# Two projections of a Trainium2 kernel: the subtraction that splits their weight chunks moves from VectorE to GpSimd

## The chip, the core and the metric

The kernel runs on one core of a Trainium2 chip. The metric is device time in microseconds (us) of one execution. The engines of the core work side by side, each through its own queue in order: TensorE (PE, matrix products, with weight loads shown as PEld), VectorE (DVE), ScalarE (ACT), GpSimd (POOL) and SyncE (SP, whose queue issues the loads from the chip's memory). They wait for each other through semaphores. SBUF is the working memory, PSUM holds what TensorE adds up.

## The reference

The program is a whole small network on 256 tokens of width 1024: two layers of attention with a feed-forward part, then a second block of two layers (mixer, cross attention, an expert layer with 128 x 128 experts). The change lies in the first of these mixers, the "even mixer". Its input `hn` is projected once and cut up; two of the parts go through a causal convolution over four tokens and a SiLU:

```python
def even_mixer(hn, w_in, w_out, ...):
    proj = hn @ w_in
    z, xbc, dt_raw, xm, og, ig, fg = jnp.split(proj, [o1, o2, o3, o4, o5, o6], axis=-1)
    y_a = ssd_mixer(z, xbc, dt_raw, ...)      # xbc: 1536 columns
    y_b = mlstm_mixer(xm, og, ig, fg, ...)    # xm: 1024 columns
    return jnp.concatenate([y_a, y_b], axis=-1) @ w_out

def ssd_mixer(...):
    xbc = jax.nn.silu(causal_conv(xbc, conv_w, conv_b))
    ...
def mlstm_mixer(...):
    xc = jax.nn.silu(causal_conv(xm, conv_w, conv_b))
    ...
```

The two projections with convolutions are `xbc` and `xm`. All of it is float32.

## The kernel before

Every large product is done in three passes. Each float32 operand is split into a rounded part `hi` and a rest `lo` (`split`, L295): ScalarE copies the operand to `hi` in TensorE's rounding format (L297), and then `lo` = operand minus `hi` is computed (L298) by the engine that is passed as `eng`, VectorE where none is passed. `mm3` (L311) issues three matmuls for each piece: `hi` by `hi` (L313), `hi` by the other side's rest (L314), and `lo` by `hi` (L315). So the third matmul is the first that needs `lo`.

Weights come in chunks of 128 x 1024 floats (512 KB). `chunk` (L300) loads one into `raw` (three buffers, L303), and splits it into `hi` and `lo` (three buffers each). A `raw` buffer is free for the next load once the subtraction has read it; `hi` and `lo` are free once TensorE has used them.

`lin_b_steps` (L344) goes through the blocks of 128 output columns: a PSUM bank, a chunk, 24 matmuls (8 pieces of the input by 3), and then a `consume` function on the result. It takes `eng` and passes it to `chunk`. For the expert layer, `eng=nc.gpsimd` is passed already (L1715, L1752).

In `even_mixer` (L1191) the first projection, `xbc`, has 12 blocks. Each is consumed by `conv` (L1177): ScalarE copies the bank to `xpad` (L1182), whose first three columns GpSimd clears (L1181), VectorE does one tensor_scalar (L1185) and three scalar_tensor_tensor steps (L1187), ScalarE a tanh (L1188), and VectorE the last product (L1189) into `xb`. Its core:

```python
nc.vector.tensor_scalar(acc, xpad[:, 3:S + 3], w(3), w("b"), op0=OP.mult, op1=OP.add)
for j in range(3):
    nc.vector.scalar_tensor_tensor(out=acc, in0=xpad[:, j:j + S], scalar=w(j), in1=acc, op0=OP.mult, op1=OP.add)
```

Between the blocks stand the softplus of small columns (L1163 to L1174) and, in `ssd` (L1260), the decay matrices `MT` (L1311) and `cme` (L1303). When all 12 are through, TensorE transposes `xb` (L1322). The projection `z` follows, then the output of the scan, and a group norm over it (L1371 to L1382) whose row goes through a small matmul (L1380, bank `rb`).

In `mlstm` (L1386) the second projection, `xm`, has 8 blocks. Each is split straight from PSUM (`xmh`, `xml`), goes through the same `conv`, and the result is split as well (`xch`, `xcl`). After it come four chunks of `og`, and the products for q, k and v (`qkp`, `vp`), whose first weight chunk is again split by VectorE. All these share four PSUM banks.

The order of the instructions in each queue is set by a scheduler when the kernel is built: it starts from the order in the code and moves an instruction forward where it expects an engine to be free. So an instruction can stand ahead of one that was written earlier. SyncE's queue holds the loads in the order of the chunks.

Of the kernel before, what the change touches and what calls it, by code (L numbers as in the profile page):

```python
# [197 lines left out]
class Net:  # L198
# [992 lines left out]
    def even_mixer(self, xp, hT):  # L1191
        nc, a = self.nc, self.a
        c = self.tables(xp, "U", "selGT")
        ident = self.ident

        sw = xp.tile([P, 192], F32, name="sw")
        nc.sync.dma_start(out=sw, in_=a["ev_sm"].rearrange("p k n -> p (k n)"))
        swh = xp.tile([P, 192], F32R, name="swh")
        swl = xp.tile([P, 192], F32R, name="swl")
        self.split(sw, swh, swl)  # L1200
        ps = self.bank("sps")
        for k in range(8):
            self.mm3(ps[0:24, 0:S], swh[:, k * 24:k * 24 + 24], swl[:, k * 24:k * 24 + 24], hT[0][:, k], hT[1][:, k], k == 0, k == 7)
        yT = self.pair(xp, "yT", 16)
        st = ExitStack()
        sp_ = st.enter_context(self.tc.tile_pool(name="ssd", bufs=1))
        xb = sp_.tile([P, 12, S], F32, name="xb")
        xbc = self.lin_b_steps(hT, a["ev_xbc"], lambda b, ps: self.conv(sp_, ps, "sconv", b, xb[:, b]),
                               [8, 9, 10, 11, 0, 1, 2, 3, 4, 5, 6, 7], bank="psb")
        self.take(xbc, 2)  # L1210
        smT = xp.tile([24, S], F32, name="smT")
        nc.scalar.copy(out=smT, in_=ps[0:24, 0:S])
        tps = self.bank("smp")
        for t in range(2):
            nc.tensor.transpose(tps[:, t * 24:t * 24 + 24], smT[:, t * P:t * P + P], ident[0:24, 0:24])
        sm = xp.tile([P, 2, 24], F32, name="smv")
        nc.vector.tensor_tensor(out=sm, in0=tps[:, 0:48].rearrange("p (t n) -> p t n", t=2),
                                in1=self.row["smb"][:, None, :].to_broadcast([P, 2, 24]), op=OP.add)
        x20 = xp.tile([P, 2, 20], F32, name="x20")
        nc.vector.tensor_copy(x20[:, :, 0:16], sm[:, :, 0:16])  # L1220
        nc.vector.tensor_scalar(x20[:, :, 16:20], sm[:, :, 16:20], -1.0, None, op0=OP.mult)
        spl = self.softplus(xp, x20.rearrange("p t n -> p (t n)"), 40).rearrange("p (t n) -> p t n", t=2)
        dt = spl[:, :, 0:16]
        na = xp.tile([P, 16], F32, name="na")
        nc.scalar.activation(out=na, in_=self.row["alog"], func=AF.Exp)
        nc.vector.tensor_scalar(na, na, -1.0, None, op0=OP.mult)
        lg = xp.tile([P, 2, 20], F32, name="lg")
        nc.vector.tensor_tensor(out=lg[:, :, 0:16], in0=dt, in1=na[:, None, :].to_broadcast([P, 2, 16]), op=OP.mult)
        nc.vector.tensor_scalar(lg[:, :, 16:20], spl[:, :, 16:20], -1.0, None, op0=OP.mult)
        self.take(xbc, 3)  # L1230
        cps = self.bank("cps")
        for t in range(2):
            nc.tensor.matmul(cps[:, t * 20:t * 20 + 20], lhsT=c["U"], rhs=lg[:, t], start=True, stop=True)
        nc.tensor.matmul(cps[:, 40:60], lhsT=self.ones, rhs=lg[:, 0], start=True, stop=True)
        cs = xp.tile([P, 3, 20], F32, name="cs")
        nc.vector.tensor_copy(cs, cps[:, 0:60].rearrange("p (t n) -> p t n", t=3))

        acc = [[self.bank("eacc") for _ in range(2)] for _ in range(2)]

        def project():  # L1240
            for kt in range(16):
                hi, lo = self.chunk(a["ev_out"][kt].rearrange("p k n -> p (k n)"), 1024)
                for t in range(2):
                    for n in range(2):
                        self.mm3(acc[t][n], yT[0][:, kt, t * P:t * P + P], yT[1][:, kt, t * P:t * P + P],
                                 hi[:, n * 512:n * 512 + 512], lo[:, n * 512:n * 512 + 512], kt == 0, kt == 15)
                yield 1
        out = project()
        self.gain_ahead("norm_xattn_2_0")
        with st:  # L1250
            self.ssd(sp_, c, hT, dt, cs, lg, yT, xb, xbc)
        with ExitStack() as st:
            sp_ = st.enter_context(self.tc.tile_pool(name="mls", bufs=1))
            self.mlstm(sp_, c, hT, sm, cs, yT, out)
        self.take(out)
        for t in range(2):
            for n in range(2):
                self.add_h(n, t, acc[t][n])
# [127 lines left out]
    def mlstm(self, pl, c, hT, sm, cs, yT, out):  # L1386
        nc, a = self.nc, self.a
# [10 lines left out]
        with self.tc.tile_pool(name="mlx", bufs=1) as px:  # L1398
            xc = self.pair(px, "xc", 8)
            xm = self.pair(px, "xm", 8)  # L1400

            def cxm(b, ps):
                self.split(ps, xm[0][:, b], xm[1][:, b])
                y = px.tile([P, S], F32, tag="xcf", name="xcf", bufs=2)
                self.conv(px, ps, "mconv", b, y)
                self.split(y, xc[0][:, b], xc[1][:, b])
            self.lin_b(hT, a["ev_xm"], cxm, bank="psb")
            self.take(og, 4)
            for hp in range(2):
                for s, dst, scl in (("q", qT, 1.0), ("k", kT, 1.0 / 16)):  # L1410
                    hi, lo = self.chunk(a[f"ml_w{s}"][hp].rearrange("p h k n -> p (h k n)"), 1024)
                    for j in range(2):
                        h = 2 * hp + j
                        ps = self.bank("qkp")
                        for e in range(2):
                            for k in range(2):
                                o = (j * 2 + k) * 256 + e * P
                                self.mm3(ps[:, e * S:e * S + S], hi[:, o:o + P], lo[:, o:o + P], xc[0][:, 2 * h + k], xc[1][:, 2 * h + k],
                                         k == 0, k == 1)
                        nc.scalar.mul(out=dst[:, 2 * h:2 * h + 2].rearrange("p e n -> p (e n)"), in_=ps, mul=scl)  # L1420
                hi, lo = self.chunk(a["ml_wv"][hp].rearrange("p h k n -> p (h k n)"), 1024)
                for j in range(2):
                    h = 2 * hp + j
                    ps = self.bank("vp")
                    for t in range(2):
                        for k in range(2):
                            o = (j * 2 + k) * 256
                            sl = slice(t * P, t * P + P)
                            self.mm3(ps[:, t * S:t * S + S], xm[0][:, 2 * h + k, sl], xm[1][:, 2 * h + k, sl], hi[:, o:o + 256],
                                     lo[:, o:o + 256], k == 0, k == 1)  # L1430
                    nc.vector.tensor_copy(v[:, :, h, 0:256], ps.rearrange("p (t n) -> p t n", t=2))
# [522 lines left out]
```

## Time and profile before

| | us |
|---|---|
| three timed runs | 3366.87, 3373.19, 3374.19 (median 3373.19) |
| the profiled execution, its own time | 3366.57 |
| its span, first to last instruction | 3364.8 |
| TensorE busy in it | 3272.0 (97%) |
| VectorE busy | 2243.8 (67%) |
| ScalarE busy | 1755.5 (52%) |
| GpSimd busy | 322.3 (10%) |

The profile is one execution. A "busy" engine has an instruction under way; an instruction that has begun and can't go on counts as busy too. "Idle before" is the time in which an engine waited ahead of an instruction, with the one that released it. The granted clock is TensorE's, as a share of its full 2.4 GHz. Shares over the whole span are averages over many stages, so a change in one stage has to be read in that stage, by window.

### The profile page before, as it was taken

To read this page: it belongs to the slowest core of one execution; us is meant where nothing else is said; L and a number is where in the kernel's file an instruction comes from. 1 tells how busy PE (TensorE), PEld (TensorE's weight loads), DVE (VectorE), ACT (ScalarE), POOL (GpSimd) and SP (SyncE) were. 2 spreads that over 40 slices of the span, in tenths; PEclk is the share of its full clock that TensorE was granted. 3 is DMA by queue.
4 is the path that set the end of the run, shared out by engine and by line. 5 is a ranking of instruction groups with operands and counts; after the bars stand their busy time and mean duration, and the time that the engine had idled before them with its cause. 6 is when DMAs were issued, how large, how long until landed. Compare 5 with 4: busy or idle time off the path is not lost. (4 is left out here: it accounts for less than half of the span.)

```text
span 3364.8 us, 54101 instructions
## 1 busy us (share of the span) xinstructions
PE 3272.0 (97%) x20874; PEld 2883.3 (86%) x20874; DVE 2243.8 (67%) x3999; ACT 1755.5 (52%) x3219; POOL 322.3 (10%) x197
## 2 busy tenths in 40 slices
PE   8999999999999999999999999999999999999999
PEld 7678998677998888898988999988889898899998
DVE  7676556666557776599955555567649996555555
ACT  4555445554446554345944444456444595444444
POOL 0000000000000000374000000000027600000000
PEclk9999999999999999999999999999999999999999
DMA  6435666444555345453255555555545415555555
GB/s 194 143 126 185 221 200 201 141 143 167 188 186 182 124 155 187 154 170 122 82 192 187 189 187 187 187 198 170 182 144 169 139 63 188 189 187 188 188 188 175
DMA packets 161108, 569.49 MB, mean 169 GB/s; under 512 B 18257, under 2 KB 23761, under 8 KB 159826
## 3 DMA queue, kind: packets, MB, share of 16 engines
q1 hardware_dynamic: 160562, 565.91, 50.4%
q8 instruction: 163, 2.67, 0.3%
q14 instruction: 95, 0.78, 0.1%
q10 hardware_dynamic: 288, 0.13, 0.0%
HBM read 556.53 MB, written 9.44 MB: 168 GB/s over the span
## 5 line engine op out<-in xcount | busy, mean ns | idle before, releaser
L298 DVE TENSOR_TENSOR lo<-raw,hi 128x1024 fp32r<-128x1024 f32 (+2 forms) x868 | 1056.0, 1218 | 723.9 <-ACT hi L297 718.8
L297 ACT CAST hi<-raw 128x1024 fp32r<-128x1024 f32 (+1 forms) x978 | 1020.7, 1044 | 916.2 <-issue 213.2
L313 PE MATMUL pacc<-hi,pwh 128*128 128x512 f32 x1024 | 404.3, 395 | 0.1
L315 PE MATMUL pacc<-hi,pwl 128*128 128x512 f32 x1024 | 403.6, 394 | 0.0
L314 PE MATMUL pacc<-lo,pwh 128*128 128x512 f32 x1024 | 402.8, 393 | 0.0
L313 PE MATMUL aps<-xTh,hi 128*128 128x256 f32 x1248 | 351.6, 282 | 1.9 <-ACT G L1796 1.9
L314 PE MATMUL aps<-xTl,hi 128*128 128x256 f32 x1248 | 351.5, 282 | 0.0
L315 PE MATMUL aps<-xTh,lo 128*128 128x256 f32 x1248 | 350.2, 281 | 0.0
L313 PE MATMUL ps<-xTh,hi 128*128 128x256 f32 x1008 | 289.3, 287 | 3.7 <-DVE xTl L298 2.8
L298 POOL TENSOR_TENSOR lo<-raw,hi 128x1024 fp32r<-128x1024 f32 x110 | 271.4, 2470 | 213.6 <-ACT hi L297 210.0
L314 PE MATMUL ps<-xTl,hi 128*128 128x256 f32 x1008 | 287.9, 286 | 1.2 <-DVE xTl L298 1.2
L315 PE MATMUL ps<-xTh,lo 128*128 128x256 f32 x1008 | 287.7, 286 | 0.0
L297 ACT CAST pwh<-G 128x256 fp32r<-128x256 f32 x256 | 103.8, 406 | 343.1 <-DVE G L1801 205.8
L313 PEld LDWEIGHTS aps<-xTh,hi 128*128 128x128 f32 x1248 | 234.7, 188 | 8.5 <-ACT G L1796 2.3
L314 PEld LDWEIGHTS aps<-xTl,hi 128*128 128x128 f32 x1248 | 234.7, 188 | 6.9
L315 PEld LDWEIGHTS aps<-xTh,lo 128*128 128x128 f32 x1248 | 234.7, 188 | 0.0
L315 PEld LDWEIGHTS pacc<-hi,pwl 128*128 128x128 f32 x1024 | 192.5, 188 | 45.5 <-DVE pwl L298 0.3
L313 PEld LDWEIGHTS pacc<-hi,pwh 128*128 128x128 f32 x1024 | 192.7, 188 | 38.7 <-ACT pwh L297 1.0
L314 PEld LDWEIGHTS pacc<-lo,pwh 128*128 128x128 f32 x1024 | 193.2, 189 | 38.0
L448 POOL TENSOR_TENSOR r<-v,mhalf 128x1 f32<-128x1 f32 x24 | 19.7, 824 | 1987.6 <-DVE v L446 1987.6
L313 PE MATMUL fps<-fTh,hi 128*128 128x256 f32 x704 | 198.5, 282 | 0.6 <-ACT fTh L297 0.4
L314 PE MATMUL fps<-fTl,hi 128*128 128x256 f32 x704 | 198.3, 282 | 0.3
(673 smaller groups left out, 7161.4 us busy)
## 6 DMA issues: line engine op xcount, KB each, us to landing
raw<-in_pu_dram SPq DMA_DIRECT2D x256, 512.0 KB, 3.3
raw<-in_pv_dram SPq DMA_DIRECT2D x256, 512.0 KB, 3.3
raw<-in_wbg_dram SPq DMA_DIRECT2D x48, 512.0 KB, 3.6
raw<-in_ffg_dram SPq DMA_DIRECT2D x44, 512.0 KB, 3.4
raw<-in_ffu_dram SPq DMA_DIRECT2D x44, 512.0 KB, 3.4
raw<-in_ffd_dram SPq DMA_DIRECT2D x44, 512.0 KB, 3.8
raw<-in_win_dram SPq DMA_DIRECT2D x36, 512.0 KB, 3.6
raw<-in_pwq_dram SPq DMA_DIRECT2D x32, 512.0 KB, 3.3
```

Source lines behind the costliest of these rows:

```text
L297: self.nc.scalar.copy(out=hi, in_=src)
L298: (eng or self.nc.vector).tensor_tensor(out=lo, in0=src, in1=hi.bitcast(F32), op=OP.subtract)
L313: mm(ps, lhsT=lh, rhs=rh, start=start, stop=False)
L314: mm(ps, lhsT=lh, rhs=rl, start=False, stop=False)
L315: mm(ps, lhsT=ll, rhs=rh, start=False, stop=stop)
L448: nc.gpsimd.tensor_tensor(out=r, in0=v, in1=self.mhalf[:, :1], op=OP.pow)
```

## The change

Both calls pass `eng=nc.gpsimd`. Nothing else is edited.

```diff
         xbc = self.lin_b_steps(hT, a["ev_xbc"], lambda b, ps: self.conv(sp_, ps, "sconv", b, xb[:, b]),
-                               [8, 9, 10, 11, 0, 1, 2, 3, 4, 5, 6, 7], bank="psb")
+                               [8, 9, 10, 11, 0, 1, 2, 3, 4, 5, 6, 7], bank="psb", eng=nc.gpsimd)
...
-            self.lin_b(hT, a["ev_xm"], cxm, bank="psb")
+            self.lin_b(hT, a["ev_xm"], cxm, bank="psb", eng=nc.gpsimd)
```

So 20 subtractions (12 and 8) change their engine, and the scheduler sets the order anew around them. On GpSimd, at the start of the first projection (`xpad` is the convolution's input, cleared in its first columns; `r` and `w` belong to the norm ahead):

```order
 L489 TENSOR_TENSOR w<-u,mhalf 128x1 x2
-L1181 MEMSET xpad 128x3 x12
+L1181 MEMSET xpad 128x3 x2
+L298 TENSOR_TENSOR lo<-raw,hi 128x1024 x4
+L1181 MEMSET xpad 128x3
+L298 TENSOR_TENSOR lo<-raw,hi 128x1024
+L1181 MEMSET xpad 128x3
+L298 TENSOR_TENSOR lo<-raw,hi 128x1024 x2
```

The queue that held only the 12 clearings now has the subtractions between them, four of them ahead of the third clearing.

On VectorE at the same place (`cacc` is the convolution's sum, `smv`, `x_10623` and `sp_a` are the softplus's columns, `mTl` an earlier split):

```order
 L298 TENSOR_TENSOR mTl<-raw,mTh 128x1024 x2
-L298 TENSOR_TENSOR lo<-raw,hi 128x1024 x2
+L1185 TENSOR_SCALAR cacc<-xpad,cl 128x256
 L1217 TENSOR_TENSOR smv<-smp,rw 128x48
+L1187 SCALAR_TENSOR_TENSOR cacc<-xpad,cl,cacc 128x256
 L1220 COPY x_10623<-smv 128x2x16
 L1221 TENSOR_SCALAR x_10623<-smv 128x2x4
-L298 TENSOR_TENSOR lo<-raw,hi 128x1024
-L1185 TENSOR_SCALAR cacc<-xpad,cl 128x256
```

The first convolution moves ahead, into the places of the subtractions.

On VectorE in the group norm ahead of the second projection (`gn_*` are its rows, `rb` the bank with its result):

```order
 L1371 TENSOR_SCALAR gn_v<-vps 2x256
-L298 TENSOR_TENSOR lo<-raw,hi 128x1024
 L1374 TENSOR_TENSOR gn_u<-gn_y 2x256
 L1375 TENSOR_TENSOR gn_u<-gn_u,gn_v 2x256
 L1376 TENSOR_SCALAR gn_u<-gn_u 2x256
-L298 TENSOR_TENSOR lo<-raw,hi 128x1024
 L1377 TENSOR_TENSOR gn_y<-gn_y,gn_u 2x256
```

The first two subtractions of the second projection leave this chain; they now stand in GpSimd's queue.

## Rows read from the trace of the kernel before

**Rows 1.** the page: busy us (share) xcount; costliest groups as busy, mean ns | idle
```profile
PE 3272.0 (97%) x20874; PEld 2883.3 (86%) x20874; DVE 2243.8 (67%) x3999; ACT 1755.5 (52%) x3219; POOL 322.3 (10%) x197
L298 POOL TENSOR_TENSOR lo<-raw,hi 128x1024 fp32r<-128x1024 f32 x110 | 271.4, 2470 | 213.6 <-ACT hi L297 210.0
```

**Rows 2.** busy us by window; columns window, length, PE, PEld, DVE, ACT, POOL, clock, DMA
```profile
1069.00:1125.40 56.40, 52.77 (x436) 51.50 (x437) 51.99 (x114) 33.48 (x78) 1.45 (x10) 1.00 0.48 159
1170.80:1210.30 39.50, 34.01 (x230) 30.85 (x231) 37.58 (x83) 23.59 (x50) 0.96 (x10) 0.96 0.42 147
```

**Rows 3.** timeline, GpSimd: start, us, engine line op, [idle before <-releaser]
```profile
1414.32 2.38 POOL L298 TENSOR_TENSOR lo<-raw,hi 128x1024 fp32r<-128x1024 f32 x1 [0.49 <-ACT hi L297]
...
2594.13 2.40 POOL L298 TENSOR_TENSOR lo<-raw,hi 128x1024 fp32r<-128x1024 f32 x1 [0.36 <-ACT hi L297]
2596.98 2.56 POOL L298 TENSOR_TENSOR lo<-raw,hi 128x1024 fp32r<-128x1024 f32 x1 [0.45 <-ACT hi L297]
```

**Rows 4.** timeline, VectorE, beside those three
```profile
1415.04 0.29 DVE L1871 MAX8 G<-rsc 128x8 f32<-128x128 f32 x1
...
2594.18 2.43 DVE L1909 TENSOR_SCALAR G<-G 128x128 uint32<-128x128 uint32 x1
2597.21 2.49 DVE L1921 SCALAR_TENSOR_TENSOR G<-G 128x128 f32<-128x128 f32 x1
```

**Rows 5.** line L1921: count, duration ns min/median/max, first and last start
```profile
L1921 DVE SCALAR_TENSOR_TENSOR G<-G x128: 275/282/2497, 1490.7 to 2671.9; 128x128 f32<-128x128 f32 x128
```

**Rows 6.** VectorE groups, 1069 to 1125.4 us: xcount | busy, mean ns | idle
```profile
L298 DVE TENSOR_TENSOR lo<-raw,hi 128x1024 fp32r<-128x1024 f32 x15 | 18.3, 1221 | 3.8 <-ACT hi L297 3.7
L1281 DVE COPY cb<-cbp 128x512 f32<-128x512 f32 x1 | 0.7, 683 | 0.0
L1273 DVE COPY bt<-btp 128x256 f32<-128x256 f32 x1 | 0.4, 417 | 0.0
```

**Rows 7.** VectorE groups, 1170.8 to 1210.3 us
```profile
L298 DVE TENSOR_TENSOR lo<-raw,hi 128x1024 fp32r<-128x1024 f32 x11 | 13.4, 1219 | 0.0
L1382 DVE SCALAR_TENSOR_TENSOR xb<-xb,cl,rb 128x256 f32<-128x256 f32 x8 | 3.4, 476 | 1.3 <-PE rb L1380 1.3
L298 DVE TENSOR_TENSOR xml<-psb,xmh 128x256 fp32r<-128x256 f32 x8 | 3.2, 417 | 0.0
```

**Rows 8.** timeline, VectorE, last convolution of the first projection
```profile
1124.96 0.43 DVE L1189 SCALAR_TENSOR_TENSOR xb<-xpad,cacc 128x256 f32<-128x256 f32 x1
```

**Rows 9.** timeline, TensorE, the transposes that read all convolutions
```profile
1128.07 2.04 PE L1322 MATMUL xsp<-cst,xb 128*128 128x128 f32 x16
```

**Rows 10.** timeline, VectorE, group norm ahead of the second projection
```profile
1167.78 0.28 DVE L1376 TENSOR_SCALAR gn_u<-gn_u 2x256 f32<-2x256 f32 x1
1167.98 1.21 DVE L298 TENSOR_TENSOR lo<-raw,hi 128x1024 fp32r<-128x1024 f32 x1
1169.12 0.41 DVE L1377 TENSOR_TENSOR gn_y<-gn_y,gn_u 2x256 f32<-2x256 f32 x1
```

**Rows 11.** timeline, ScalarE, same place
```profile
1166.75 1.04 ACT L297 CAST hi<-raw 128x1024 fp32r<-128x1024 f32 x1
```

**Rows 12.** timeline, TensorE, same place
```profile
1169.67 0.67 PE L1380 MATMUL rb<-gn_y,cst 2*128 2x256 f32 x2 [0.92 <-DVE gn_y L1377]
```

**Rows 13.** timeline, VectorE, end of the second projection
```profile
1210.21 1.22 DVE L298 TENSOR_TENSOR lo<-raw,hi 128x1024 fp32r<-128x1024 f32 x1
```

**Rows 14.** timeline, TensorE, the matmul that reads that tile
```profile
1213.30 0.28 PE L315 MATMUL qkp<-xch,lo 128*128 128x256 f32 x1
```

**Rows 15.** TensorE waits, 1060 to 1130 us: us in total, times, longest
```profile
PE psb L315 <- DVE lo L298: 3.6, 3, 1.8
```

**Rows 16.** TensorE waits, 1165 to 1215 us
```profile
PE psl L314 <- DVE lo L298: 2.3, 1, 2.3
PE psl L313 <- ACT xpad L1182: 1.7, 1, 1.7
```

**Rows 17.** busy us by window, 1200 to 1220 us
```profile
1200.00:1220.00 20.00, 19.25 (x105) 16.45 (x105) 13.76 (x23) 11.78 (x20) 0.20 (x2) 0.91 0.58 192
```

## The prediction

> **What bounds the kernel now.** I read the page first, for the share of each engine. TensorE is busy 97% of the span, GpSimd 10%; one subtraction of a weight chunk on GpSimd, as it stands elsewhere in this kernel, takes 2.47 us [rows 1]. So the kernel is near TensorE's limit, and a change elsewhere counts only where TensorE waits. Then I cut out the two stretches that are touched, by window. In stretch A, from the first matmuls of the first projection to the end of its last convolution (1069.0 to 1125.4 us), TensorE is busy 52.77 of 56.40 us and VectorE 51.99; in stretch B, from the second projection until the last convolution there is split (1170.8 to 1210.3 us), 34.01 and 37.58 of 39.50 us [rows 2]. In both, VectorE is as full as TensorE or fuller. That is the reader's first finding: relief for VectorE would matter here, and a further load on it would as well. TensorE's waits name its share: 3.6 us for `lo` in A [rows 15]; in B 2.3 us for `lo` and 1.7 us for a bank that a ScalarE copy has to clear [rows 16], after which the granted clock of 1200 to 1220 us is 0.91, so some matmuls ran at the lower of the two levels [rows 17].
>
> Last I looked up how GpSimd's subtraction and VectorE get on where they already run together, in the expert layer. A VectorE tensor_scalar of 128x128 begins 0.05 us after a GpSimd `lo` and takes 2.43 us, to that subtraction's end; the next one of that kind under a `lo`, a scalar_tensor_tensor, takes 2.49 us [rows 3, 4]. Over its 128 executions that scalar_tensor_tensor has a median of 0.282 us and a maximum of 2.497 us [rows 5]. It isn't slower by a share: it stands still until GpSimd is done. A MAX8, which reads one tensor, ran in 0.29 us in the middle of another `lo` [rows 3, 4].
>
> **The change part by part.** Twelve chunks of the first projection and eight of the second lose a VectorE subtraction of 1.22 us each [rows 6, 7] and get one of 2.47 us on GpSimd [rows 1]. No DMA, no ScalarE cast and no matmul is added. The wait of each L315 matmul, and the release of each `raw` buffer, moves from VectorE to GpSimd.
>
> The question is what VectorE can do during those 2.47 us. The convolution (L1185 to L1189), the softplus, the products with `cb` and `ex`, and the splits of `yT` and `xc` read two tensors from SBUF or are tensor_scalars from SBUF to SBUF: the kinds that stood still in rows 4. Some operations read PSUM and at most one tensor in SBUF (`cb`, `bt`, `xml`, L1382). No row shows one of these under a GpSimd `lo`; MAX8 is the nearest, so I let them run, and keep the other case as a bound.
>
> Stretch A. VectorE's 51.99 us less 12 x 1.221 = 14.65 us leaves 37.3 us [rows 2, 6]. Of this 1.5 us read PSUM (`cb` 0.7, `bt` 0.4 [rows 6], and two small ones of 0.2). So 35.8 us want the shared path, and GpSimd wants 12 x 2.47 = 29.6 us of it. One after the other that is 65.4 us from 1068.9: 1134.3 us. In between the path is idle at times: VectorE was idle 4.4 us of this stretch before, mostly at its start, where the first two GpSimd subtractions now fit in; I add 2 of the 4.4. The last convolution then ends near 1136.3 instead of 1125.4 us [rows 8], 10.9 us later. TensorE needs it at 1128.07, at the transposes of L1322 [rows 9], so 2.7 us are swallowed: +8.2 us. Ends: if nothing stands still, two of the three waits on `lo` go (2.7 of 3.6 us) and the first chunk's `lo` comes 1.2 us later: -1.5 us. If all 12 hold VectorE for their whole length, 12 x 1.25 = 15 us, and the 2.7 us are gone for other reasons: +15 us.
>
> Ahead of stretch B the group norm loses two subtractions from VectorE's row. The second one stood between L1376 and L1377, from 1167.98 for 1.21 us [rows 10]. Without it L1377 could start 1.1 us sooner. But ScalarE's cast for that chunk ends at 1167.79 [rows 11], GpSimd starts then or behind L1376 at 1168.0, and L1377, which reads two SBUF tensors, stands still to 1170.4 and ends at 1170.8 instead of 1169.53. The matmul of L1380 waits for it already [rows 12]: +1.3 us. If it slips in first: -0.9 us, the wait in rows 12.
>
> Stretch B. VectorE's 37.58 us less six subtractions, 6 x 1.22 = 7.3 us, leaves 30.3 us, of which 3.4 (L1382) and 3.2 us (`xml`) read PSUM [rows 2, 7]. So 23.7 us want the path, and GpSimd 6 x 2.47 = 14.8 us: 38.5 us if those 6.6 us all fit beside GpSimd, 45.1 us if none does, against 37.58: +0.9 to +7.5, middle 4.2 us. At the end VectorE's `lo` of the next projection is done at 1211.4 [rows 13], and TensorE reads it at 1213.30 [rows 14], so 1.9 us are swallowed. Together 1.3 + 4.2 - 1.9 = +3.6 us. Ends: -7 us without any standstill (next part but one), and 1.3 + 7.5 = +8.8 us.
>
> What the VectorE rows say of the order: the scheduler moves convolutions forward into the places that are left. In GpSimd's queue the clearing of `xpad` now stands behind subtractions, so the first convolution of B waits until the fifth subtraction is done. This is inside the sum above, since the path is held in that time anyway.
>
> One rule of the notes bears on this. The Trainium skill, "SBUF — State Buffer", section "Who interferes with whom", says that VectorE shares its second SBUF port with GpSimd, that an operation with two SBUF inputs or in a two-port mode and a GpSimd operation that reads SBUF exclude each other for the whole instruction, and that one with a single SBUF input doesn't contend. The trace agrees with the first two (2.43 and 2.49 us in rows 4) and with the third for MAX8. By its last part alone stretch B would be at its lower value, 0.9 instead of 4.2 us, and the sum at +8.5 us.
>
> **Sum.** 8.2 + 3.6 = 11.8, some +12 us. The profiled execution took 3366.57 us by its own time, with a span of 3364.8 us; the three timed runs lie at 3366.87, 3373.19 and 3374.19 us, their median 6.6 us above the profiled one. On the profiled execution the sum gives 3378.4, on the median 3385.0; I take the middle, 3382 us. Between TensorE's stretches and the end everything hangs on the buffers and not on a fixed hour, so I let the delay go through to the end whole.
>
> **The rivals.**
> Faster: the standstill of rows 4 belongs to the operations of that layer, and the convolution's don't stand still. Then TensorE's waits go: 1.5 us in A; in B 0.9 (rows 12), 2.3 and 1.7 (rows 16), and the clock's 9% of 20 us, 1.8 us (rows 17), less a `lo` that is late for want of a cast, 1 us: about 7 us there. 8 us in all, 3362 us. For it: B's waits are VectorE's lateness, and 20 x 1.22 us are much relief. Against it: rows 4 and 5. The place is the convolution in both stretches; the point from which it decides is a subtraction that holds VectorE for less than half of its 2.47 us, since VectorE paid 1.22 us for it before.
>
> Hidden: VectorE is late, but three weight buffers and four PSUM banks let TensorE run ahead, and the transposes at L1322 can be reached with less delay than I think; the relief in B pays for A. 0 to +5 us, 3372 us. For it: TensorE reached L1322 2.7 us after the last convolution as it was [rows 8, 9], and it is idle only 3.6 of 56.4 us in A [rows 2]. Against it: the transposes need every convolution, and 10.9 us are four times that slack.
>
> Worse: GpSimd has its next operands ready whenever it ends, so VectorE gets an operation or two between subtractions, casts that stand behind ScalarE's tanh come late, and TensorE's longer waits end at the lower clock as in rows 17. Then A costs 15 and B 8.8 us, and two more such falls of the clock 3.6 us: +27 us, 3397 us.
>
> **How the numbers follow.** About 0.2%, 6.7 us, is what a measurement of this kernel can tell from no change. Forecast (the shared path decides, +5 to +22 us): 0.55. Worse: 0.13. Hidden: 0.19. Faster: 0.13. So faster 0.13, same 0.19, slower 0.68. The range that holds 8 in 10: from 3365, which leaves most of the faster case out, to 3400 us, which takes the worse one in; the forecast's own range is 3375 to 3392 us.
>
> **What would show it.** Right: under a GpSimd `lo` the convolution's operations in the new profile have durations up to some 2.5 us beside a usual 0.4 to 0.5; the last L1189 of A ends near 1136; TensorE has a new wait of 5 to 9 us at L1322 and a wait for `gn_y` near 2 us. Wrong: L1187 keeps its mean near 0.48 us in A; then the faster rival holds. If the means rise but TensorE shows no wait at L1322, the delay is hidden. If TensorE waits for GpSimd's `lo` at most chunks, the queue order on GpSimd and ScalarE is the bound, not the path.

## The result and the profile after

The changed kernel takes 3395.95 us in the median of five runs (3391.03 to 3401.22), the kernel before 3373.19 us in five runs beside it. The ratio is 1.0078, with an interval of 1.0066 to 1.0090: 26 us slower. The profiled execution has a span of 3389.3 us against 3364.8, 24.5 us more. The two stretches and the sign are the ones that the prediction named, and the time lies inside its whole range (3365 to 3400 us). But the loss is more than twice the +12 us of the sum and above the forecast's own +5 to +22 us, and the first stretch costs more than twice what it said.

I split the spans by five marks on TensorE: the first matmul of the first projection, the first and the last of the eight decay blocks (`csb`, L1305), the transposes of L1322 and the first `rwb` matmul.

| us between marks | before | after | more |
|---|---|---|---|
| first matmul to first `csb` | 23.90 | 38.31 | 14.4 |
| first to last `csb` | 28.48 | 35.61 | 7.1 |
| last `csb` to L1322 | 6.80 | 6.80 | 0 |
| L1322 to `rb` (L1380), with the group norm | 41.60 | 42.72 | 1.1 |
| `rb` to `rwb`, with stretch B | 60.41 | 64.17 | 3.8 |

The first three rows are stretch A: 59.18 before, 80.72 after. It begins 0.9 us earlier and the rest of the span is 1.1 us shorter, so 26.4 of the marks become the 24.5 of the span.

Stretch A of the kernel after, by window (window, length, busy us of TensorE, weight loads, VectorE, ScalarE, GpSimd, then clock, DMA share and GB/s); it ends with the last convolution:

```profile
1068.02:1146.31 78.29, 60.42 (x438) 57.59 (x439) 60.26 (x102) 32.86 (x78) 29.98 (x22) 0.87 0.35 115
```

Against [rows 2], VectorE has 12 subtractions less and is busy 8 us longer, and TensorE's mean clock fell from 1.00 to 0.87. VectorE's groups in this stretch (count, busy us, mean ns, idle before and who ended it) show where VectorE's time went, first those of before, 1069 to 1125.4 us, then those of after, 1068 to 1146.3 us:

```profile
L1187 DVE SCALAR_TENSOR_TENSOR cacc<-xpad,cl,cacc 128x256 f32<-128x256 f32 x36 | 17.2, 479 | 0.3
...
L1185 DVE TENSOR_SCALAR cacc<-xpad,cl 128x256 f32<-128x256 f32 x12 | 4.9, 409 | 0.0
```

```profile
L1187 DVE SCALAR_TENSOR_TENSOR cacc<-xpad,cl,cacc 128x256 f32<-128x256 f32 x36 | 23.4, 650 | 1.1
L1185 DVE TENSOR_SCALAR cacc<-xpad,cl 128x256 f32<-128x256 f32 x12 | 16.4, 1370 | 11.7 <-ACT xpad L1182 11.7
...
L1169 DVE TENSOR_TENSOR sp_z<-sp_z 128x40 f32<-128x40 f32 x1 | 2.4, 2415 | 0.0
```

The same 48 steps of the convolution take 39.8 us where they took 22.1, and one 128x40 step of the softplus takes 2.4 us. One decay block of after, the engines together (start, us, engine, line, operation, idle before):

```profile
1118.47 0.42 ACT L1188 ACTIVATE xpad<-cacc 128x256 f32<-128x256 f32 x1 [3.49 <-DVE cacc L1187]
1118.79 1.03 ACT L297 CAST hi<-raw 128x1024 fp32r<-128x1024 f32 x1
...
1119.90 2.38 POOL L298 TENSOR_TENSOR lo<-raw,hi 128x1024 fp32r<-128x1024 f32 x1 [0.34 <-ACT hi L297]
...
1120.13 2.31 DVE L1185 TENSOR_SCALAR cacc<-xpad,cl 128x256 f32<-128x256 f32 x1 [0.78 <-ACT xpad L1182]
...
1122.54 1.01 DVE L1187 SCALAR_TENSOR_TENSOR cacc<-xpad,cl,cacc 128x256 f32<-128x256 f32 x2
1123.47 0.68 DVE L1311 TENSOR_TENSOR MT<-MT,cb 128x512 f32<-128x512 f32 x1
1124.07 0.48 DVE L1187 SCALAR_TENSOR_TENSOR cacc<-xpad,cl,cacc 128x256 f32<-128x256 f32 x1
1124.64 0.42 ACT L1188 ACTIVATE xpad<-cacc 128x256 f32<-128x256 f32 x1 [3.50 <-DVE cacc L1187]
```

Read it as a ring of 6.17 us (1118.47 to 1124.64): tanh, the cast that stands behind it in ScalarE's queue, GpSimd's subtraction, VectorE's scale held until the subtraction's end at 1122.28, then the convolution and the next tanh. In each ring neither GpSimd nor VectorE has anything to do for 0.54 us under the tanh and for 0.56 us until the cast is done; between the two VectorE makes the block's last product (L1189).

TensorE's waits in after, 1055 to 1150 us (us in total, times, longest), against the 3.6 us of [rows 15]:

```profile
PE cbp L1279 <- DVE xb L1189: 6.1, 1, 6.1
PE psb L315 <- POOL lo L298: 3.4, 3, 2.0
PE psb L313 <- DVE cs L1236: 3.2, 1, 3.2
PE csb L1305 <- ACT xpad L1182: 2.2, 1, 2.2
PE cso L1299 <- ACT xpad L1182: 2.0, 1, 2.0
```

The two longest lie ahead of the first decay block. `cbp` needs four finished convolutions; the other waits for a PSUM bank that the copy `cs` clears. That copy ran 1.06 us after its matmuls before (1089.27 against 1088.21) and 11 us after them now (1100.26 against 1089.30), behind nine steps of the convolutions, three of which were held for 2.3 to 2.5 us. TensorE all but stood still from 1092 us on, and its granted clock was 0.50 (1.2 GHz) and then 0.67 in the mean, so the work after the waits was slow as well (windows, columns as above):

```profile
1092.00:1100.00 8.00, 0.76 (x2) 0.50 (x2) 7.21 (x8) 1.62 (x3) 4.67 (x3) 0.50 0.39 132
1100.00:1108.00 8.00, 7.47 (x44) 7.39 (x45) 4.32 (x13) 2.76 (x8) 0.77 (x3) 0.67 0.21 68
```

The marks behind, in timelines of after; they answer to [rows 8, 9, 10, 12]:

```profile
1145.89 0.42 DVE L1189 SCALAR_TENSOR_TENSOR xb<-xpad,cacc 128x256 f32<-128x256 f32 x1
...
1148.74 1.47 PE L1322 MATMUL xsp<-cst,xb 128*128 128x128 f32 x12
...
1188.84 2.47 DVE L1377 TENSOR_TENSOR gn_y<-gn_y,gn_u 2x256 f32<-2x256 f32 x1
...
1191.46 0.88 PE L1380 MATMUL rb<-gn_y,cst 2*128 2x256 f32 x3 [1.94 <-DVE gn_y L1377]
```

### The profile page after: what moved, and what is told of

Its sections match the earlier page's. It is cut to its first block, busy times and chain, and to the rows that moved or that the text cites. A ratio compares the mean times of both kernels' runs of the same rounds, so it can differ in the third digit from the quotient of the medians.

```text
span 3389.3 us, 54096 instructions
## 1 busy us (share of the span) xinstructions
PE 3281.6 (97%) x20874; PEld 2892.5 (85%) x20874; DVE 2256.9 (67%) x3979; ACT 1753.0 (52%) x3219; POOL 371.0 (11%) x217
## 3 DMA queue, kind: packets, MB, share of 16 engines
q8 instruction: 163, 2.67, 0.3%
## 5 line engine op out<-in xcount | busy, mean ns | idle before, releaser
L298 DVE TENSOR_TENSOR lo<-raw,hi 128x1024 fp32r<-128x1024 f32 (+2 forms) x848 | 1031.7, 1218 | 720.0 <-ACT hi L297 714.4
L298 POOL TENSOR_TENSOR lo<-raw,hi 128x1024 fp32r<-128x1024 f32 x130 | 320.7, 2470 | 279.2 <-ACT hi L297 276.7
```

The source lines that it names most:

```text
L298: (eng or self.nc.vector).tensor_tensor(out=lo, in0=src, in1=hi.bitcast(F32), op=OP.subtract)
```

## The experiments

Theory: while GpSimd subtracts, VectorE's work from SBUF stands still, so the times of the two engines add up, and where a chain has nothing else to run, idle time comes on top. Rivals: the price is only GpSimd's longer subtraction, paid per chunk; or the order in ScalarE's queue. All times below are ratios times the median of the kernel before beside it (3367 to 3369 us); stage times are from the profiled executions. In stretches where the code is as before, the profiles differ little: `rb` to `rwb` takes 60.2 to 62.3 us in three kernels that leave stretch B alone, and the first matmul comes between 1068 and 1072 us. So 2 us between two profiles there are not told from none.

**One stretch at a time.**

```diff
 xbc_only, against the changed kernel:
-self.lin_b(hT, a["ev_xm"], cxm, bank="psb", eng=nc.gpsimd)
+self.lin_b(hT, a["ev_xm"], cxm, bank="psb")
 xm_only:
-        [8, 9, 10, 11, 0, 1, 2, 3, 4, 5, 6, 7], bank="psb", eng=nc.gpsimd)
+        [8, 9, 10, 11, 0, 1, 2, 3, 4, 5, 6, 7], bank="psb")
```

> Only the 12 chunks of xbc are subtracted on GpSimd, those of xm on VectorE as before. Theory (a GpSimd subtraction stops VectorE's SBUF work for its whole length, and the chain tanh, cast, subtraction, convolution lets nothing run beside it in the first stretch): +20 to +23 us, with the transposes of the first stretch some 21 us later than before and the same 6.15 us from one subtraction to the next. Rival (each subtraction is only 1.25 us longer, and that is paid per chunk): 12 of 20 chunks of the whole +26, so +15 to +16 us.

> Only the 8 chunks of xm are subtracted on GpSimd. Theory: +3 to +5 us, since in the second stretch TensorE's own work hides most of what VectorE loses. Rival (a price per chunk): 8 of 20 chunks of +26, so +10 us.

Measured: +22 us (17 to 27) with xbc alone, +6 us (3 to 9) with xm alone. Stretch A is 80.42 us with xbc alone, as with both. 12 and 8 chunks cost 1.9 and 0.8 us each, so there is no one price per chunk for both stretches. The middle of xm alone is above the 3 to 5 expected, its interval holds them.

**The first stretch cut in two.**

```diff
-hi, lo = self.chunk(..., eng=eng)
+hi, lo = self.chunk(..., eng=eng(b) if callable(eng) else eng)
 head_only: eng=lambda b: nc.gpsimd if b in (8, 9, 10, 11, 0) else None
 tail_only: eng=lambda b: None if b in (8, 9, 10, 11, 0) else nc.gpsimd
```

> Of the xbc chunks only the first five (blocks 8 to 11 and 0) are subtracted on GpSimd; the other seven and all of xm on VectorE. The comparison of the two traces puts 14.4 us of the first stretch's 21.5 between the first chunk and the first decay matrix (softplus, four convolutions, cs and cbp stand behind one another), and 7.1 us into the eight decay blocks that follow. Theory (the standstill is paid where a chain has nothing else to run): +11 to +16 us, with the transposes of the first stretch 12 to 16 us late. Rival (price per subtraction): 5 of 12 of +22, so +9 us.

> The other half: the first five xbc chunks on VectorE, the last seven on GpSimd, xm on VectorE. Theory: the time to the first decay matrix is as before, and what is left is the ring of the decay blocks, +4 to +9 us. Rival (price per subtraction): 7 of 12 of +22, so +13 us.

Measured: +5 us (2 to 8) for the head, +10 us (6 to 14) for the tail. The head misses its expectation; the tail's interval reaches into 4 to 9 us, but its time to the first `csb` isn't as before. Both miss in the same way: I had put all 14.4 us ahead of the first `csb` on the first five chunks. By the marks the head costs 7.6 us there and nothing in the decay blocks (28.49 us), the tail 5.3 us there and 7.3 us in the blocks (35.80 us). Together 20.2 us, near the 21.2 of xbc alone. The tail's interval also holds the rival's +13 us, and by the marks a chunk costs 1.5 us in the head and 1.8 in the tail. So inside the first stretch these two runs don't tell a price per chunk from the theory. The tail's early loss is visible in the softplus, VectorE and then GpSimd in the tail-only kernel:

```profile
1082.10 2.38 DVE L1172 SCALAR_TENSOR_TENSOR sp_q<-sp_q,sp_z 128x40 f32<-128x40 f32 x1
...
1087.96 2.41 DVE L1174 SCALAR_TENSOR_TENSOR sp_q<-sp_q,sp_m 128x40 f32<-128x40 f32 x1
```

```profile
1081.98 2.44 POOL L298 TENSOR_TENSOR lo<-raw,hi 128x1024 fp32r<-128x1024 f32 x1
...
1087.87 2.45 POOL L298 TENSOR_TENSOR lo<-raw,hi 128x1024 fp32r<-128x1024 f32 x1
```

Two subtractions each begin just ahead of a step that takes 0.19 us by itself, and hold the chain that `cps` waits for by 2.2 us each; `cps` comes 4.9 us later after the first matmul than before (24.24 against 19.32).

**GpSimd beside VectorE's own subtraction: reading, and only writing.** The chunk's `lo` still comes from VectorE.

```diff
+if beside:   # beside_read
+    self.nc.gpsimd.tensor_tensor(out=src, in0=src, in1=hi.bitcast(F32), op=OP.subtract)
+if beside:   # beside_write
+    for n in (1024, 1024, 512):
+        self.nc.gpsimd.memset(src[:, 0:n], 0.0)
```

> As the kernel before: VectorE subtracts all chunks. Behind each of the 20 subtractions GpSimd makes the same subtraction again, 128x1024 with two SBUF inputs, and writes it over the raw chunk, which nobody reads any more. Nothing waits for GpSimd but the next load into that raw buffer. Theory (VectorE stands still while GpSimd reads SBUF): VectorE's 50.4 us of work in the first stretch and 29.6 us of GpSimd come one after the other, at least 80 us where there were 56, so with the second stretch +30 to +50 us. Rival (only the latency of GpSimd in the chain counts): 0 to +4 us.

> As the one before, but GpSimd only writes: three memsets (1024, 1024 and 512 columns, estimated at 2.3 us together from the 128x2048 memset of 1.82 us and the 128x512 one of 0.52 us) into the raw chunk behind each of VectorE's 20 subtractions. Theory (the standstill comes from GpSimd reading SBUF beside VectorE): -1 to +5 us, with convolution steps as short as before. If any GpSimd work stops VectorE, or if the later release of the raw buffers is the price: as much as the run with the reading subtraction.

Measured: +35 us (30 to 40) reading, +10 us (7 to 14) writing. The first speaks for the theory and against the latency of the chain (0 to +4 us), since no matmul waits for GpSimd's subtraction here. More than the next load stands behind GpSimd, the clearing of `xpad` too; but VectorE was busy for 75.32 of the 77.7 us from 1068.28 to 1146, so it hardly waited for that. Stretch A takes 80.12 us, and in those 77.7 us VectorE and GpSimd's subtractions, laid over one another from their timelines, leave 0.2 us in which neither works: VectorE always has something to do, and the path alone sets the length. That stretch A is about as long as in the changed kernel is chance: there the path is 11 us shorter, and 11.75 us are idle. The writing run missed its expectation. VectorE's groups in stretch A of the writing run:

```profile
L1191 DVE SCALAR_TENSOR_TENSOR cacc<-xpad,cl,cacc 128x256 f32<-128x256 f32 x36 | 17.0, 475 | 0.2
L1189 DVE TENSOR_SCALAR cacc<-xpad,cl 128x256 f32<-128x256 f32 x12 | 9.8, 817 | 0.0
```

The steps with two inputs are as before, the scale from SBUF to SBUF took twice its time. Of the 10 us only 3 are in stretch A (62.13 us); 7.5 are in `rb` to `rwb`, where the clock was 0.90 between 1170 and 1240 us against 0.98. How the scale's 0.4 us would become that much there isn't shown.

**The convolution from PSUM.**

```diff
-nc.vector.tensor_scalar(acc, xpad[:, 3:S + 3], w(3), w("b"), ...)
+nc.vector.tensor_scalar(acc, ps, w(3), w("b"), ...)
-    nc.vector.scalar_tensor_tensor(out=acc, in0=xpad[:, j:j + S], scalar=w(j), in1=acc, ...)
+    nc.vector.scalar_tensor_tensor(out=acc[:, d:], in0=ps[:, 0:S - d], scalar=w(j), in1=acc[:, d:], ...)  # d = 3 - j
```

> The partner: the same convolution from PSUM with the subtraction on VectorE. It is the base of the run with GpSimd; against the kernel before -8 to +10 us, since a ScalarE copy per block goes and the PSUM bank is held through four VectorE steps. All theories expect the same here.

> All 20 chunks on GpSimd as in the changed kernel, but the convolution reads its input from PSUM (no copy into a padded SBUF tile, no memset): its scale reads PSUM alone, its three shifted steps read PSUM and one SBUF tile; the last step still has two SBUF inputs. Theory (what GpSimd stops is VectorE work that has two SBUF inputs or a fast SBUF mode): the convolution is no longer stopped, and the kernel is within -2 to +6 us of its partner with the same convolution and VectorE's subtraction, with the scale at 0.4 us where it was 1.4. Rival (queue order, or the longer chain of cast and subtraction): +20 to +26 us above the partner, as in the changed kernel.

> The convolution that reads PSUM with VectorE's subtraction, and behind each of the 20 subtractions the three memsets of GpSimd into the raw chunk. In the run with memsets beside the old convolution only its first step (a scale from SBUF to SBUF) grew, from 0.41 to 0.82 us. If that was the price of a writing GpSimd (the scale now reads PSUM and does not stand still): 0.52 to 0.56 us for the scale and -3 to +4 us against the partner without memsets. If it was the later release of the raw buffers, or GpSimd's writing as such: +8 to +12 us, as there.

Measured: +1 us (-2 to 4) with VectorE's subtraction, +13 us (9 to 18) with GpSimd's, +1 us (-2 to 4) with VectorE's and the memsets. In the last the scale takes 538 ns beside the memsets, and the 10 us are gone: a writing GpSimd as such, or the later release of the raw buffers, isn't their price. The scale from SBUF to SBUF is the one step of the old convolution that the memsets were seen to stop. That it alone made the 10 us isn't shown, since this convolution also drops the copy and the clearing of `xpad`. Against its partner the run with GpSimd is 13 us slower, half of the 26: more than the 6 that the theory allowed and less than the rival's 20, so neither range held. The two profiled spans differ by 8.9 us. VectorE's groups of the run with GpSimd, 1068 to 1146 us:

```profile
L1310 DVE TENSOR_TENSOR MT<-MT,cb 128x512 f32<-128x512 f32 x8 | 9.5, 1188 | 0.2 <-ACT MT L1309 0.2
...
L1182 DVE TENSOR_SCALAR cacc<-psb,cl 128x256 f32<-128x256 f32 x12 | 6.4, 536 | 9.9 <-PE psb L315 9.8
...
L1185 DVE SCALAR_TENSOR_TENSOR cacc<-psb,cl,cacc 128x255 f32<-128x255 f32 x12 | 5.8, 480 | 0.2
...
L1169 DVE TENSOR_TENSOR sp_z<-sp_z 128x40 f32<-128x40 f32 x1 | 2.4, 2440 | 0.0
L1170 DVE TENSOR_SCALAR sp_q<-sp_z 128x40 f32<-128x40 f32 x1 | 2.3, 2304 | 0.0
```

and of its partner:

```profile
L1182 DVE TENSOR_SCALAR cacc<-psb,cl 128x256 f32<-128x256 f32 x12 | 6.5, 539 | 0.6 <-PE psb L315 0.6
L1185 DVE SCALAR_TENSOR_TENSOR cacc<-psb,cl,cacc 128x255 f32<-128x255 f32 x12 | 5.7, 478 | 0.0
...
L1310 DVE TENSOR_TENSOR MT<-MT,cb 128x512 f32<-128x512 f32 x8 | 5.5, 685 | 0.1
```

The steps that read PSUM run through; the product with `cb` (1188 against 685 ns) and the softplus, which read SBUF, are held. The decay blocks lose nothing (28.47 us in both kernels, 28.48 before), with ScalarE's cast behind its tanh and GpSimd's whole subtraction as in the changed kernel, so GpSimd's latency by itself costs nothing there. This convolution also takes the clearing of `xpad` out of GpSimd's queue; the next pair of runs shows what such an order is worth. What is left of A's loss, 8.1 us, lies ahead of the first `csb` (32.18 against 24.08 us), and 1.0 at the group norm. How much of the 8.1 us is the held softplus, and how much the longer way through GpSimd or the clock, no run tells apart.

The Trainium skill, "SBUF — State Buffer", section "Who interferes with whom", says that an instruction with at most one SBUF input outside the two-port modes doesn't contend, that one with two SBUF inputs contends with a GpSimd that reads but not with one that only writes, and that a tensor_scalar can be in a two-port mode and then contends. The trace agrees in all three: 480 against 478 ns for the steps from PSUM; 650 ns beside subtractions and 475 beside memsets, against 479, for those with two SBUF inputs; 817 against 409 ns for the scale.

**The order of the queues.** The tanh of a block takes its zero bias from the next chunk's cast, so that the cast stands ahead of it; then the padding is also cleared once.

```diff
+nxt = get(blocks[i + 1])   # cast and subtraction of the next chunk, ahead of consume(b)
+nc.scalar.mul(out=zb, in_=nh[:, 0:1].bitcast(F32), mul=0.0)
-nc.scalar.activation(out=xpad[:, 3:S + 3], in_=acc, func=AF.Tanh)
+nc.scalar.activation(out=xpad[:, 3:S + 3], in_=acc, func=AF.Tanh, bias=zb)
 (cast_ahead_pads also: two fixed xpad tiles, cleared once)
```

> The changed kernel with the cast of the next xbc chunk made to stand ahead of the tanh of this block in ScalarE's queue (the tanh takes its zero bias from a tiny product with that chunk's cast). GpSimd's subtraction still stands behind the memset that waits for the last step of the convolution. Theory (a ring of waits around a path that one engine at a time uses): the subtraction begins only about 0.34 us earlier per block, as the memset now lets it go; first stretch about 4 us shorter than in the changed kernel, whole +20 to +24 us. Rival (ScalarE's queue order alone made the loss): the loss of the first stretch goes, whole +4 to +10 us.

> As the one before, and the padding columns are set once per stretch (two fixed tiles), so that no memset stands ahead of GpSimd's subtractions. Theory: VectorE and GpSimd now hand the path to one another without idle time, 2.4 us of subtraction and 2.9 us of VectorE work per block, 5.3 us where the changed kernel has 6.15; over 12 blocks 10 us less, whole +13 to +18 us. It does not fall to the kernel before, because the path itself is longer. Rival (order of the queues is the whole loss): -2 to +5 us. Rival (latency of GpSimd per chunk): no change, +24 to +27 us.

Measured: +23 us (19 to 28) for both. The decay blocks take 32.92 and 32.88 us instead of 35.61, 2.7 less where about 4 and 10 were expected; the time to the first `csb` is unchanged (38.21, 38.37). So queue order is worth 2.7 us in the decay blocks. The second run misses its 13 to 18 us, and its interval holds the 24 to 27 of the rival that GpSimd's latency is the price; against that rival stand the run with the reading subtraction and the decay blocks of the convolution from PSUM. In the second run the subtractions do run ahead, but they hold other steps instead, as VectorE's groups (1068 to 1146 us) show:

```profile
L1207 DVE SCALAR_TENSOR_TENSOR cacc<-xpad,cl,cacc 128x256 f32<-128x256 f32 x36 | 27.8, 773 | 0.6
L1213 DVE SCALAR_TENSOR_TENSOR xb<-xpad,cacc 128x256 f32<-128x256 f32 x11 | 8.0, 725 | 5.6 <-ACT xpad L1212 5.4
L1205 DVE TENSOR_SCALAR cacc<-xpad,cl 128x256 f32<-128x256 f32 x12 | 6.8, 563 | 7.1 <-ACT xpad L1202 7.1
```

From the first matmul to the last convolution, VectorE or a GpSimd subtraction is at work for 66.5 us both here and in the changed kernel (75.50 us less 9.05 in which neither works, and 78.29 less 11.75): another order doesn't shorten the path, and most of the idle time, which the second run was to remove, stayed.

**Half a chunk each.** The edit also reached the 110 chunks that the kernel before already subtracts on GpSimd.

```diff
+for e, s in ((eng, slice(0, 512)), (self.nc.vector, slice(512, 1024))):
+    e.tensor_tensor(out=lo[:, s], in0=src[:, s], in1=hi[:, s].bitcast(F32), op=OP.subtract)
```

> The changed kernel with each of the 20 subtractions cut in two: columns 0 to 511 on GpSimd, 512 to 1023 on VectorE. Theory (GpSimd's time and VectorE's add up on one path): per chunk 1.24 us of GpSimd and 0.62 us of VectorE, 1.86 us on the path where the changed kernel has 2.47 and the kernel before 1.22. The first stretch loses 0.64 us for each of 12 chunks (7.7 us) and some of the idle time of the changed kernel, 8 to 14 us; whole +12 to +19 us. Rival (the two halves run side by side and the split is done after 1.24 us, as long as VectorE alone takes): -2 to +3 us.

Measured: +50 us (45 to 56), of which 41.6 lie behind the `rwb` mark, at those other chunks, so the total says nothing of this change. Stretch A alone is 65.74 us, 6.6 more than before, a little under the 8 to 14 expected, against 21.5 with whole chunks. GpSimd's groups, 1068 to 1146 us:

```profile
L302 POOL TENSOR_TENSOR lo<-raw,hi 128x512 fp32r<-128x512 f32 x12 | 18.2, 1520 | 10.6 <-ACT hi L297 9.4 <-DMA raw<-in_ev_xbc_dram 1.1
```

1.52 us for half the columns is more than half of 2.47. Where VectorE's half began just ahead of it (1074.06 and 1074.11 us), GpSimd's took 1.79 us; without VectorE's half beside it, at 1082.18, it took 1.29. So the halves got in each other's way, as the theory has it.

No version here is faster than the kernel before.

## Why the prediction was right, and where it was wrong

**The time: inside the range, but by the room left for a rival.** +12 us and 3382 were forecast, +26 (22 to 30) and 3395.95 came, above the forecast's own 3392. The range reached to 3400 only to take in Worse, which had a chance of 0.13. So the kind of loss and its stretches were foreseen, its size was not; that the time fell into the range was partly luck.

**Standstill: right.** The question what VectorE can do during GpSimd's 2.47 us was answered as the rows of the expert layer had it, and MAX8's case carried over to the steps that read PSUM: two of the L1382 steps ran in 0.48 and 0.47 us under a `lo` (1192.59 and 1192.99 us). beside_read, and the pair with the convolution from PSUM, show the rest; the Faster rival falls. (Its terms for stretch B add up to 5.7 us, not to about 7; nothing hung on it.)

**Stretch A, "I add 2 of the 4.4": wrong, the largest error.** The path's own time was well sized: 65.4 us predicted, 66.5 measured. The idle time between its pieces was 11.75 us. Its larger gaps stand at the first two chunks (2.6 us), around `cb` and the first decay block (3.3) and at four rings of the decay blocks (1.0 to 1.1 each). Carrying over VectorE's idle time of before supposed that the path could always be filled. But one chunk's chain holds the next one's cast, and the softplus, the convolutions and `cs` are one chain with TensorE waiting at its end.

**"So 2.7 us are swallowed": wrong.** The distance from the last L1189 to L1322 stayed, 2.67 us before and 2.43 after (1146.31 to 1148.74), and the last `csb` to L1322 is 6.80 us in both. TensorE had been held earlier, at `cbp`, at banks and by the clock, so it arrived as late as the convolution did. The difference of 8.2 and 21.5 us is made up by these: 9.75 of idle time, 1.1 of path, 2.4 of slack. 21.5 lies outside the ends that I gave A (-1.5 to +15): the upper end counted only longer subtractions.

**"A new wait of 5 to 9 us at L1322": wrong place.** There is none; the waits are 6.1 us at `cbp` and 3.2 at a bank.

**Group norm: right. Stretch B: near in size.** L1377 took 2.47 us, as worked out, TensorE waited 1.94 us for it, and the way to `rb` took 1.1 us longer (1.3 predicted). With B it makes 4.9 us in the profile and 6 (3 to 9) in xm alone, against 3.6; the profile of xm alone has 7.6. Whether B's part came by the path, as predicted, isn't shown: TensorE's longest waits there are now 2.2 us for GpSimd's `lo` and 1.8 for L1382.

**The rivals.** Hidden falls. Worse had +27 us, which is the size that came, but with 15 us in A and 8.8 in B where it was 21.5 and 3.8. Its casts behind the tanh are in the rows, and cast_ahead prices them at 2.7 us in the decay blocks; its low clock is there too. How much of the 14.4 us ahead of the first `csb` is the clock, and how much VectorE's new order (its first scale now stands ahead of the softplus and waits 7.1 us), wasn't told apart.

## What to carry to other kernels

Before work goes from VectorE to GpSimd, sort VectorE's neighbours by operands: beside a GpSimd subtraction, those that read PSUM and at most one SBUF tensor ran on, and those that read two SBUF tensors or scale SBUF to SBUF waited for its end, however small they were. Add the two engines' times as one path, and then walk the chain once around (who waits for the held step, and what that releases) before any idle time or slack is carried over from the old profile. If VectorE must run beside GpSimd, let its inputs stay in PSUM: that took the loss of the decay blocks away altogether, though 13 of the 26 us stayed.

## What was not expected of the hardware

A GpSimd that only writes also holds VectorE's scale from SBUF to SBUF (817 against 409 ns), and no other step of the convolution. GpSimd is held by VectorE too. In the run with the reading subtraction, GpSimd and then VectorE in stretch B:

```profile
1220.94 4.58 POOL L301 TENSOR_TENSOR raw<-raw,hi 128x1024 f32<-128x1024 f32 x1 [5.50 <-ACT xpad L1191]
```

```profile
1220.72 0.75 DVE L1192 SCALAR_TENSOR_TENSOR xcf<-xpad,cacc 128x256 f32<-128x256 f32 x2
1221.39 1.22 DVE L299 TENSOR_TENSOR lo<-raw,hi 128x1024 fp32r<-128x1024 f32 x1
1222.53 0.75 DVE L299 TENSOR_TENSOR xcl<-xcf,xch 128x256 fp32r<-128x256 f32 x2
1223.20 4.93 DVE L1188 TENSOR_SCALAR cacc<-xpad,cl 128x256 f32<-128x256 f32 x2
```

The subtraction lasted 4.58 us, where the 20 of its kind have a median of 2.49, while VectorE's steps with two SBUF inputs ran on without a break to 1223.28. The next scale was in turn held until the subtraction's end at 1225.52.
